# Attention with a threshold on the weights: a float32 screen without a norm check, GpSimd with DMA alone, flags and split in one instruction each

## The chip, the cores and the metric

The kernel runs on one core of a Trainium2 chip. The metric is the device time of one execution in microseconds, as the median of several runs. A NeuronCore has TensorE (PE, with its weight loads as PEld), VectorE (DVE), ScalarE (ACT), GpSimd (POOL) and SyncE (SP), which work side by side, each through its instructions in order, and wait for one another by semaphores. [...]

## The reference

```
Q, K, V: (8, 12, 512, 64) float32, normally distributed; threshold = 0.1
scores  = einsum('bhqd,bhkd->bhqk', Q, K) / sqrt(64)
weights = softmax(scores)
weights = where(weights > threshold, weights, 0)
weights = weights / (sum(weights) + 1e-10)
out     = einsum('bhqk,bhkd->bhqd', weights, V)
```

A query row in which no weight is over 0.1 gives a row of zeros.

## The kernel before

Two heads make a pair, and there are 48 pairs. A tile of a pair has 128 partitions; Q and K of both heads lie side by side as 128 columns, 4 rows a partition. SyncE first writes zeros into the whole output of a pair (L173). The kernel then screens all query rows at low cost, finds those in which a weight can pass the threshold, and computes only these rows exactly and writes them over the zeros.

A pair goes through these steps, in five turns of the loop over pairs:

1. *Load and transpose.* `do_load` fetches Q, K and V (three pairs ahead). `do_tr` (L182) transposes Q and K by 4 float32 matmuls each; ScalarE takes Q out of PSUM as bf16 (`do_qev`, L188) and K as float32 with its row sums (`do_kev`, L194); VectorE writes 512 times K minus its sum as bf16 (`do_kcentre`, L200).
2. *Screen.* Four steps `g` a pair: `do_qk` (L231) makes the scores of 128 rows of both heads by two matmuls, head 0 on rows 0 to 63 of the array, head 1 on rows 64 to 127. `do_screen` gives head 0 to ScalarE, a sum of exponentials (L243), and head 1 to VectorE, a maximum (L245).
3. *Norms.* GpSimd squares the bf16 Q and K (`do_squares`, L208), TensorE sums the squares (`do_norms`, L217), ScalarE keeps them (`do_normev`, L222). At the end the largest norm tells whether the bf16 screen's margin was wide enough.
4. *Select.* `do_flags` (L250, L251) compares sums and maxima with a cut. `do_rank` (L259, L261) counts flagged rows by matmuls, `do_key` and `do_idx` turn the counts into row numbers, and `do_gather` (L287) fetches up to 64 rows of each head by an indirect DMA of GpSimd.
5. *Exact rows.* `do_split` (L297, two instructions) puts the rows of the two heads into separate columns, `do_xtr` (L303) transposes, `do_xqk` (L314) makes float32 scores, `do_xexp` (L320) the exponentials, `do_xmask` (L326, L328) the threshold, `do_xpt` (L336) the transpose of the weights, `do_xptev` (L342) its eviction by ScalarE, `do_xpv` (L351) the product with V, whose 65th column of ones gives the sum; `do_xout` scales (L358 to L361) and scatters the rows by an indirect DMA of GpSimd (L362). V is cast to bf16 by VectorE (`do_vcast`, L177).

The order of each engine is the program's own: every instruction is pinned by `keep(...)`, and the loop over `g` at the end of the function writes the steps of five pairs in one fixed order, by `qi`, the step within the pair. For pair `hp`, TensorE's order is: score pair 0, rank of `hp-1`, transposes of Q of `hp+1`, L314 of `hp-3`, score pair 1, transposes of K of `hp+1`, L351 of `hp-4`, score pair 2, row numbers of `hp-1`, score pair 3, L303, L336, norms. The scores, the transposes and L314 share 5 PSUM buffers (`spsum`).

If more than 64 rows of a head are flagged, or a norm is too large, a slow loop at the end (L465 on) computes everything; it is not entered here.

Of the kernel before, what the change touches and what calls it, by code (L numbers as in the profile page):

```python
# [11 lines left out]
def kernel(  # L12
# [33 lines left out]
    DV = D + 1  # L46
# [15 lines left out]
    SCREEN = mybir.dt.bfloat16  # L62
    NORM_CAP = 160.0

    MARGIN = 1.05 * NORM_CAP * 2.0 ** -8 * scale + 0.005
# [80 lines left out]
    load = ctx.enter_context(tc.tile_pool(name="load", bufs=5))  # L146
    tpool = ctx.enter_context(tc.tile_pool(name="t", bufs=3))
# [9 lines left out]
    q_in, k_in, v_in, q_t, k_t, kc_t = {}, {}, {}, {}, {}, {}  # L157
# [4 lines left out]
    def load_pair(q_sb, k_sb, v_sb, hp):  # L162
        for dst, src in ((q_sb, Qf), (k_sb, Kf)):
            for h2 in range(2):
                nc.sync.dma_start(out=dst[:, :, h2 * D:(h2 + 1) * D], in_=src[hp][:, :, h2, :])
        nc.sync.dma_start(out=v_sb[:], in_=Vf[hp])

    def do_load(hp):
        q_sb = load.tile([P, SO, 2 * D], f32)
        k_sb = load.tile([P, SO, 2 * D], f32)  # L170
        v_sb = load.tile([P, 2, SO, D], f32)
        load_pair(q_sb, k_sb, v_sb, hp)
        nc.sync.dma_start(out=Oz[hp], in_=zero[:])  # L173
        q_in[hp], k_in[hp], v_in[hp] = q_sb, k_sb, v_sb

    def do_vcast(hp):
        keep(nc.vector.tensor_copy(v_bufs[hp % NV][:, :, :, 0:D], v_in.pop(hp)[:]))  # L177

# [7 lines left out]
    def do_qev(hp, sc):  # L186
        qt = tpool.tile([P, SO * P], SCREEN)
        keep(nc.scalar.copy(qt[:], sc[:]))  # L188
        q_t[hp] = qt

    def do_kev(hp, sc):
# [19 lines left out]
    def do_norms(hp):  # L211
        nm = mpsum.tile([P, P], f32, name="sm")
        for which in range(2):
            sq = sq_t.pop((hp, which))
            for r in range(SO):
                c = (which * SO + r) * 2
                keep(nc.tensor.matmul(nm[:, c:c + 2], lhsT=sq[:, r * P:(r + 1) * P], rhs=heads[:],  # L217
                                      start=True, stop=True))
        nm_t[hp] = nm

    def do_normev(hp):
        keep(nc.scalar.copy(norms[:, hp].rearrange("p w c -> p (w c)"), nm_t.pop(hp)[:, 0:4 * SO]))  # L222
# [3 lines left out]
    def do_qk(g):  # L226
        hp, qi = divmod(g, SO)
        for h2 in range(2):
            sc = spsum.tile([P, SO * P], f32)
            ps = slice(h2 * D, (h2 + 1) * D)  # L230
            keep(nc.tensor.matmul(sc[:], lhsT=q_t[hp][ps, qi * P:(qi + 1) * P],  # L231
                                  rhs=kc_t[hp][ps, :], start=True, stop=True))
            sc_t[g, h2] = sc

    def do_screen(g):
        hp, qi = divmod(g, SO)
        if qi == 0:
            sums = small.tile([P, SO], f32)
            tops = small.tile([P, SO], f32)
            st_t[hp] = sums, tops  # L240
        sums, tops = st_t[hp]
        junk = junkp.tile([P, SO * P], bf16)
        keep(nc.scalar.activation(junk[:], sc_t.pop((g, 0))[:], ACTF.Exp, scale=BETA * scale / CS,  # L243
                                  accum_out=sums[:, qi:qi + 1]))
        keep(nc.vector.tensor_reduce(tops[:, qi:qi + 1], sc_t.pop((g, 1))[:], axis=AX.X, op=ALU.max))  # L245
# [47 lines left out]

    def do_split(hp):
        qb = work.tile([P, 2 * D], f32)
        for h2 in range(2):
            keep(nc.vector.tensor_scalar(qb[:, h2 * D:(h2 + 1) * D], qsel_bufs[hp % NS][:],  # L297
                                         half[:, h2:h2 + 1], None, op0=ALU.mult))
        qb_t[hp] = qb

    def do_xtr(hp):
        xp = mpsum.tile([P, P], f32, name="sm")
        keep(nc.tensor.matmul(xp[:], lhsT=qb_t.pop(hp)[:], rhs=identity_f32[:],  # L303
# [36 lines left out]
    def do_xptev(hp):  # L340
        pt = work.tile([P, SO, P], bf16)
        keep(nc.scalar.copy(pt[:], ptp_t.pop(hp)[:]))  # L342
        pts_t[hp] = pt

    def do_xpv(hp):
        pt = pts_t.pop(hp)
        o = mpsum.tile([P, P], f32, name="sm")
        for h2 in range(2):
            sl = slice(h2 * SLOTS, (h2 + 1) * SLOTS)
            for kj in range(SO):  # L350
                keep(nc.tensor.matmul(o[sl, 0:DV], lhsT=pt[:, kj, sl], rhs=v_bufs[hp % NV][:, h2, kj, :],  # L351
                                      start=(kj == 0), stop=(kj == SO - 1)))
        o_t[hp] = o
# [188 lines left out]
```

## Time and profile before

| | us |
|---|---|
| median of 3 runs | 572.74 |
| lowest, highest | 569.52, 573.75 |
| the profiled execution | 567.96 |
| its span in the profile | 566.2 |

The profile is of one execution. Busy time is given by engine and line; the idle time before an instruction is put down to what released it. A time in order of time counts from the span's start. TensorE's ends are modelled, and GpSimd's spans are rough.

### The profile page before, as it was taken

The numbers are of one execution on the slowest core, as the hardware profiler recorded it, in microseconds if no ns is written. First come the engines' busy times: TensorE is split into PE (matmuls) and PEld (weight loads), VectorE is DVE, ScalarE is ACT, GpSimd is POOL, SyncE is SP. The second block draws the span as 40 slices with busy tenths as digits, with TensorE's granted clock in tenths as the row PEclk, the third lists the DMA queues.
The fourth block names the chain that finished last, engine by engine and source line by source line (L and its number), as shares of the span: only waits on it lengthen the run. The fifth ranks groups of instructions, "written<-read, shape, count | busy, mean of one in ns | idle before, by whom it ended". The sixth has DMA issues, their size and how long they took to land. (4 is left out here: it accounts for less than half of the span.)

```text
span 566.2 us, 7626 instructions
## 1 busy us (share of the span) xinstructions
PE 353.7 (62%) x2258; PEld 180.1 (32%) x2258; DVE 396.6 (70%) x873; ACT 255.5 (45%) x769; POOL 202.1 (36%) x224
## 2 busy tenths in 40 slices
PE   4766665675666656567665775667565775567561
PEld 2332333233333332333332332333232333233220
DVE  2866778577777776786787667776777678766841
ACT  4544544454445434544544445435544454444430
POOL 5432344223433432352244223432334224432421
PEclk9766566666665666766566657566756656665655
DMA  7982444244344333433432244334433342000000
GB/s 196 264 203 69 114 114 115 68 117 102 78 106 119 81 78 92 125 89 88 120 97 79 78 121 106 79 76 108 115 84 77 87 117 64 23 21 4 2 6 3
DMA packets 124460, 52.13 MB, mean 92 GB/s; under 512 B 104764, under 2 KB 118272, under 8 KB 124416
## 3 DMA queue, kind: packets, MB, share of 16 engines
q1 hardware_dynamic: 121344, 50.35, 34.0%
q0 software_dynamic: 3072, 1.27, 1.3%
q8 instruction: 19, 0.31, 0.2%
q14 instruction: 25, 0.20, 0.1%
HBM read 39.32 MB, written 14.16 MB: 94 GB/s over the span
## 5 line engine op out<-in xcount | busy, mean ns | idle before, releaser
L245 DVE TENSOR_REDUCE tops<-sc 128x1 f32<-128x512 f32 x192 | 131.7, 686 | 135.0 <-PE sc L231 135.0
L287 POOL DMA_INDIRECT qsel<-in_Q_dram,idx x48 | 51.6, 1074 | 288.2 <-DVE idx L286 228.6
L243 ACT ACTIVATE junk<-sc 128x512 bf16<-128x512 f32 x192 | 114.0, 600 | 75.2 <-PE sc L231 75.1
L251 DVE TENSOR_SCALAR f<-tops 128x4 bf16<-128x4 f32 x48 | 115.6, 2408 | 0.0
L231 PE MATMUL sc<-kc,qt 64*128 64x512 bf16 x384 | 100.8, 518 | 2.3 <-DVE kc L200 2.3
L314 PE MATMUL sc<-kt,xq 128*128 128x512 f32 x96 | 92.5, 1067 | 0.0
L188 ACT CAST qt<-sc 128x512 bf16<-128x512 f32 x48 | 28.1, 586 | 125.5 <-PE sc L182 125.5
L303 PE MATMUL sm<-identity_f,qb 128*128 128x128 f32 x48 | 21.0, 438 | 88.4 <-DVE qb L297 82.9
L259 PE MATMUL sm<-f,tri 128*128 128x8 bf16 x48 | 9.0, 188 | 100.1 <-DVE f L251 100.1
L362 POOL DMA_INDIRECT out_dram<-res,idx x48 | 48.7, 1015 | 59.0 <-ACT xq L309 47.0
L182 PE MATMUL sc<-identity_f,q_sb 128*128 128x128 f32 x192 | 52.5, 429 | 4.9 <-POOL qsel L143 4.9
L208 POOL TENSOR_TENSOR sq<-qt 128x512 bf16<-128x512 bf16 x48 | 50.3, 1048 | 4.4 <-ACT qt L188 3.2
L208 POOL TENSOR_TENSOR sq<-kc 128x512 bf16<-128x512 bf16 x48 | 50.0, 1041 | 2.8 <-DVE kc L200 2.8
L182 PE MATMUL sc<-identity_f,k_sb 128*128 128x128 f32 x192 | 46.1, 385 | 0.5 <-DMA k_sb<-in_K_dram 0.5
L231 PEld LDWEIGHTS <-qt 64*128 64x128 bf16 x384 | 19.6, 98 | 76.2 <-issue 72.5
L259 PEld LDWEIGHTS <-tri 128*128 128x128 bf16 x48 | 5.0, 104 | 120.5 <-DVE f L251 119.4
L303 PEld LDWEIGHTS sm<-identity_f,qb 128*128 128x128 f32 x48 | 8.2, 171 | 104.8 <-DVE qb L297 102.9
L309 ACT COPY xq<-sm 128x128 f32<-128x128 f32 x48 | 12.8, 266 | 60.4 <-PE sm L303 60.4
L243 ACT ACTIVATION_READ_ACCUMULATOR junk<-sc 128x1 f32 x192 | 39.1, 204 | 0.0
L328 DVE SCALAR_TENSOR_TENSOR m<-e,tv 128x512 bf16<-128x512 f32 x48 | 36.1, 751 | 1.7
L182 PEld LDWEIGHTS sc<-identity_f,k_sb 128*128 128x128 f32 x192 | 30.4, 196 | 19.6 <-issue 19.2
L182 PEld LDWEIGHTS sc<-identity_f,q_sb 128*128 128x128 f32 x192 | 34.4, 217 | 5.3 <-POOL qsel L143 4.9
(63 smaller groups left out, 464.4 us busy)
## 6 DMA issues: line engine op xcount, KB each, us to landing
q_sb<-in_Q_dram SPq DMA_DIRECT2D x96, 128.0 KB, 3.5
k_sb<-in_K_dram SPq DMA_DIRECT2D x96, 128.0 KB, 3.3
v_sb<-in_V_dram SPq DMA_DIRECT2D x48, 256.0 KB, 3.5
out_dram<-zero SPq DMA_DIRECT2D x48, 256.0 KB, 3.3
qsel<-in_Q_dram,idx POOLq DMA_INDIRECT x48, 4.6
out_dram<-res,idx POOLq DMA_INDIRECT x48, 2.2
```

What stands on the lines that cost most here:

```text
L182: keep(nc.tensor.matmul(sc[:, r * P:(r + 1) * P], lhsT=src[:, r, :], rhs=identity_f32[:], is_transpose=True, start=True, stop=True))
L188: keep(nc.scalar.copy(qt[:], sc[:]))
L208: keep(nc.gpsimd.tensor_tensor(out=sq[:], in0=src[:], in1=src[:], op=ALU.mult))
L231: keep(nc.tensor.matmul(sc[:], lhsT=q_t[hp][ps, qi * P:(qi + 1) * P], rhs=kc_t[hp][ps, :], start=True, stop=True))
L243: keep(nc.scalar.activation(junk[:], sc_t.pop((g, 0))[:], ACTF.Exp, scale=BETA * scale / CS, accum_out=sums[:, qi:qi + 1]))
L245: keep(nc.vector.tensor_reduce(tops[:, qi:qi + 1], sc_t.pop((g, 1))[:], axis=AX.X, op=ALU.max))
L251: keep(nc.vector.tensor_scalar(f[:, 1, :], tops[:], CUT * CS / scale, None, op0=ALU.is_gt))
L287: keep(nc.gpsimd.indirect_dma_start(out=qsel_bufs[hp % NS][:], out_offset=None, in_=Qr, in_offset=bass.IndirectOffsetOnAxis(ap=idx[:, 0:1] ...
L303: keep(nc.tensor.matmul(xp[:], lhsT=qb_t.pop(hp)[:], rhs=identity_f32[:], is_transpose=True, start=True, stop=True))
L314: keep(nc.tensor.matmul(sc[:], lhsT=xq_t.pop(hp)[:], rhs=k_t.pop(hp)[:], start=True, stop=True))
L328: keep(nc.vector.scalar_tensor_tensor(out=m[:], in0=e[:], scalar=tv[:, 0:1], in1=e[:], op0=ALU.is_gt, op1=ALU.mult))
L362: keep(nc.gpsimd.indirect_dma_start(out=Or, out_offset=bass.IndirectOffsetOnAxis(ap=ix_t.pop(hp)[:, 0:1], axis=0), in_=res[:], in_offset=N ...
```

## The change

- The screen's Q and centred K become float32 and lie in one tile `qk`; the score matmuls are float32. The margin of the cut is 0.01, and the norms, their squares and their check at the end are left out.
- GpSimd's loop holds only DMAs: the gather, the scatter, and a DMA that loads V two pairs ahead and casts it to bf16 (`do_vload`). SyncE no longer loads V, VectorE no longer casts it.
- The screen of step 3 is done by ScalarE for both heads, so VectorE takes 3 maxima a pair instead of 4, ScalarE 5 exponentials instead of 4.
- The flags are one comparison of two tiles, the split one product of two broadcast tiles.
- The eviction of the transposed weights goes from ScalarE to VectorE, the scaling of the result from VectorE to ScalarE.
- V has no column of ones any more: four more matmuls with one column each make the sum.

```diff
...
-    SCREEN = mybir.dt.bfloat16
-    NORM_CAP = 160.0
-
-    MARGIN = 1.05 * NORM_CAP * 2.0 ** -8 * scale + 0.005
+    SCREEN = f32
+    MARGIN = 0.01
...
+    cuts = consts.tile([P, 2, SO], f32)
+    nc.gpsimd.memset(cuts[:], CUT_SUM)
+    nc.gpsimd.memset(cuts[:, 1, 0:SO - 1], CUT * CS / scale)
...
+    vpool = ctx.enter_context(tc.tile_pool(name="v", bufs=8))
...
-        nc.sync.dma_start(out=v_sb[:], in_=Vf[hp])
+
+    def do_vload(hp):
+        v_bf = vpool.tile([P, 2, SO, D], bf16)
+        keep(nc.gpsimd.dma_start(out=v_bf[:], in_=Vf[hp]))
+        v_in[hp] = v_bf
...
-    def do_vcast(hp):
-        keep(nc.vector.tensor_copy(v_bufs[hp % NV][:, :, :, 0:D], v_in.pop(hp)[:]))
...
-        qt = tpool.tile([P, SO * P], SCREEN)
-        keep(nc.scalar.copy(qt[:], sc[:]))
-        q_t[hp] = qt
+        qk = tpool.tile([P, 2, SO * P], SCREEN)
+        keep(nc.scalar.copy(qk[:, 0, :], sc[:]))
+        qk_t[hp] = qk
...
-    def do_squares(hp, which):
-        sq = work.tile([P, SO * P], bf16, name=f"sq{which}")
-        src = q_t[hp] if which == 0 else kc_t[hp]
-        keep(nc.gpsimd.tensor_tensor(out=sq[:], in0=src[:], in1=src[:], op=ALU.mult))
-        sq_t[hp, which] = sq
...
-            keep(nc.tensor.matmul(sc[:], lhsT=q_t[hp][ps, qi * P:(qi + 1) * P],
-                                  rhs=kc_t[hp][ps, :], start=True, stop=True))
+            keep(nc.tensor.matmul(sc[:], lhsT=qk_t[hp][ps, 0, qi * P:(qi + 1) * P],
+                                  rhs=qk_t[hp][ps, 1, :], start=True, stop=True))
...
+        for h2 in range(2):
+            sc = sc_t.pop((g, h2))
+            if h2 == 0 or qi == SO - 1:
+                junk = junkp.tile([P, SO * P], bf16)
+                keep(nc.scalar.activation(junk[:], sc[:], ACTF.Exp, scale=BETA * scale / CS,
+                                          accum_out=stat[:, h2, qi:qi + 1]))
+            else:
+                keep(nc.vector.tensor_reduce(stat[:, h2, qi:qi + 1], sc[:], axis=AX.X, op=ALU.max))
...
-        keep(nc.vector.tensor_scalar(f[:, 0, :], sums[:], CUT_SUM, None, op0=ALU.is_gt))
-        keep(nc.vector.tensor_scalar(f[:, 1, :], tops[:], CUT * CS / scale, None, op0=ALU.is_gt))
+        keep(nc.vector.tensor_tensor(out=f[:], in0=st_t.pop(hp)[:], in1=cuts[:], op=ALU.is_gt))
...
-        for h2 in range(2):
-            keep(nc.vector.tensor_scalar(qb[:, h2 * D:(h2 + 1) * D], qsel_bufs[hp % NS][:],
-                                         half[:, h2:h2 + 1], None, op0=ALU.mult))
+        keep(nc.vector.tensor_tensor(
+            out=qb[:], in0=qsel_bufs[hp % NS][:].unsqueeze(1).to_broadcast([P, 2, D]),
+            in1=half[:].unsqueeze(2).to_broadcast([P, 2, D]), op=ALU.mult))
...
-        keep(nc.scalar.copy(pt[:], ptp_t.pop(hp)[:]))
+        keep(nc.vector.tensor_copy(pt[:], ptp_t.pop(hp)[:]))
...
+        for kj in range(SO):
+            keep(nc.tensor.matmul(o[:, D:D + 1], lhsT=pt[:, kj, :], rhs=ones_bf[:, 0:1],
+                                  start=(kj == 0), stop=(kj == SO - 1)))
...
-        keep(nc.vector.tensor_scalar(res[:], o[:, 0:D], rcp[:, 0:1], None, op0=ALU.mult))
+        keep(nc.scalar.activation(res[:], o[:, 0:D], ACTF.Copy, scale=rcp[:, 0:1]))
...
-            if has(hp):
-                do_norms(hp)
+            if has(hp + 2):
+                do_vload(hp + 2)
...
```

VectorE, around the flags of a pair. Before, from the split (`qb`) over the scaling (`res`) and the fourth maximum (`tops`) to the two flag instructions (`f`), the next pair's first maximum and the cast of V:

```order
L297 TENSOR_SCALAR qb<-qsel_111,half 128x64 x2
L358 TENSOR_SCALAR rcp<-sm 128x1
L359 RECIPROCAL rcp<-rcp 128x1
L361 TENSOR_SCALAR res<-sm,rcp 128x64
L245 TENSOR_REDUCE tops<-sc 128x1
L250 TENSOR_SCALAR f<-sums 128x4
L251 TENSOR_SCALAR f<-tops 128x4
L245 TENSOR_REDUCE tops<-sc 128x1
L177 CAST v_one_99<-v_sb 128x8x64
```

In the changed kernel, the same place:

```order
L264 TENSOR_TENSOR qb<-qsel_93,half 128x128
L329 TENSOR_SCALAR rcp<-sm 128x1
L330 RECIPROCAL rcp<-rcp 128x1
L218 TENSOR_TENSOR f<-stat,cuts 128x8
L214 TENSOR_REDUCE stat<-sc 128x1
L310 COPY pt<-pt 128x512
```

The scaling and the fourth maximum have gone from between the reciprocal and the flags, the split and the flags are one instruction each, and the eviction of the weights (`pt`) stands where the cast of V stood.

ScalarE, from the eviction of K (`kt`) to the next pair's first screen (`junk`), before:

```order
L194 ACTIVATE kt,ksum<-sc 128x512
L320 ACTIVATE e,sum_4590<-sc 128x512
L243 ACTIVATE junk,sums<-sc 128x512 x2
L309 COPY xq<-sm 128x128
L222 COPY norms<-sm 128x16
L243 ACTIVATE junk,sums<-sc 128x512
```

In the changed kernel, from the exponentials of the exact rows (`e`) on:

```order
L288 ACTIVATE e,sum_4202<-sc 128x512
L211 ACTIVATE junk,stat<-sc 128x512
L332 ACTIVATE res<-sm,rcp 128x64
L211 ACTIVATE junk,stat<-sc 128x512 x2
L277 COPY xq<-sm 128x128
L211 ACTIVATE junk,stat<-sc 128x512
```

The scaling (`res`) now stands between the third screen and the last one, which has two instructions.

GpSimd, one pair and the start of the next, before, with the gather (`qsel`), the scatter (`out_dram`) and the squares (`sq`):

```order
L287 DMA qsel_109<-in_Q_dram,idx 128x64
L362 DMA out_dram<-res,idx 49152x64
L208 TENSOR_TENSOR sq_2448<-qt 128x512
L208 TENSOR_TENSOR sq_2480<-kc 128x512
L287 DMA qsel_111<-in_Q_dram,idx 128x64
```

In the changed kernel:

```order
L254 DMA qsel_93<-in_Q_dram,idx 128x64
L333 DMA out_dram<-res,idx 49152x64
L157 DMA v_bf<-in_V_dram 128x2x256
L254 DMA qsel_95<-in_Q_dram,idx 128x64
L333 DMA out_dram<-res,idx 49152x64
```

The load of V stands where the squares stood.

## Rows read from the trace of the kernel before

**Rows 1.** Busy time of each engine, share of the span, instructions.

```profile
PE 353.7 (62%) x2258; PEld 180.1 (32%) x2258; DVE 396.6 (70%) x873; ACT 255.5 (45%) x769; POOL 202.1 (36%) x224
```

**Rows 2.** Line L251 (min/median/max, first and last start), and the wait for it.

```profile
L251 DVE TENSOR_SCALAR f<-tops x48: 157/2768/2778, 14.9 to 538.5; 128x4 bf16<-128x4 f32 x48
...
PE sm L259 <- DVE f L251: 100.1, 45, 2.5
```

**Rows 3.** Order of time around the flags: start us, us, engine, line, operation [idle before].

```profile
308.24 1.02 POOL L362 DMA_INDIRECT out_dram<-res,idx  x1 [1.11 <-ACT xq L309]
...
308.59 2.77 DVE L251 TENSOR_SCALAR f<-tops 128x4 bf16<-128x4 f32 x1
...
309.28 1.05 POOL L208 TENSOR_TENSOR sq<-qt 128x512 bf16<-128x512 bf16 x1
...
310.28 1.04 POOL L208 TENSOR_TENSOR sq<-kc 128x512 bf16<-128x512 bf16 x1
...
311.42 0.19 PE L259 MATMUL sm<-f,tri 128*128 128x8 bf16 x1 [2.49 <-DVE f L251]
```

**Rows 4.** Order of time, flags of the last pair.

```profile
537.45 1.02 POOL L362 DMA_INDIRECT out_dram<-res,idx  x1 [0.31 <-DVE res L361]
...
538.49 0.16 DVE L251 TENSOR_SCALAR f<-tops 128x4 bf16<-128x4 f32 x1
```

**Rows 5.** Order of time, TensorE: a dense stretch, and a score pair of another.

```profile
322.90 1.09 PE L182 MATMUL sc<-identity_f,q_sb 128*128 128x128 f32 x4
323.79 1.92 PE L314 MATMUL sc<-kt,xq 128*128 128x512 f32 x2
325.63 0.61 PE L231 MATMUL sc<-kc,qt 64*128 64x512 bf16 x2
...
327.22 0.44 PE L351 MATMUL sm<-v_one,pt 128*64 128x65 bf16 x8
...
315.89 0.39 PE L231 MATMUL sc<-kc,qt 64*128 64x512 bf16 x2
```

**Rows 6.** Order of time, VectorE, from the third maximum to the reciprocal.

```profile
304.99 0.69 DVE L245 TENSOR_REDUCE tops<-sc 128x1 f32<-128x512 f32 x1 [0.74 <-PE sc L231]
...
306.96 0.41 DVE L297 TENSOR_SCALAR qb<-qsel,half 128x64 f32<-128x64 f32 x2
...
307.47 0.16 DVE L359 RECIPROCAL rcp<-rcp 128x1 f32<-128x1 f32 x1
```

**Rows 7.** Stretches: length, busy us (x) of PE, PEld, DVE, ACT, POOL; granted clock, DMA, GB/s.

```profile
299.40:305.10 5.70, 5.61 (x32) 2.83 (x32) 2.26 (x7) 2.82 (x7) 0.00 (x0) 0.50 0.40 125
305.10:308.50 3.40, 1.31 (x19) 0.83 (x17) 3.30 (x12) 1.64 (x8) 1.32 (x2) 1.00 0.49 108
308.50:312.00 3.50, 1.01 (x8) 0.59 (x7) 3.50 (x5) 0.85 (x3) 2.80 (x3) 0.50 0.03 7
...
323.60:329.00 5.40, 5.37 (x26) 2.08 (x24) 1.97 (x6) 3.44 (x10) 0.00 (x0) 0.50 0.55 153
...
14.90:538.50 523.60, 335.49 (x2162) 171.55 (x2161) 384.20 (x833) 244.33 (x742) 188.57 (x184) 0.62 0.36 94
...
315.60:316.00 0.40, 0.40 (x11) 0.31 (x10) 0.36 (x3) 0.34 (x2) 0.00 (x0) 1.00 1.06 384
```

**Rows 8.** Groups by line: busy us, mean ns | idle before; L177 as min/median/max.

```profile
L243 ACT ACTIVATE junk<-sc 128x512 bf16<-128x512 f32 x192 | 114.0, 600 | 75.2 <-PE sc L231 75.1
...
L243 ACT ACTIVATION_READ_ACCUMULATOR junk<-sc 128x1 f32 x192 | 39.1, 204 | 0.0
...
L361 DVE TENSOR_SCALAR res<-sm,rcp 128x64 f32<-128x64 f32 x48 | 13.6, 283 | 1.6
...
L177 DVE CAST v_one<-v_sb x48: 411/415/2505, 10.1 to 531.1; 128x512 bf16<-128x512 f32 x48
```

**Rows 9.** Line L328 (min/median/max ns), and a gather beside it.

```profile
L328 DVE SCALAR_TENSOR_TENSOR m<-e,tv x48: 750/752/753, 36.2 to 552.0; 128x512 bf16<-128x512 f32 x48
...
306.07 1.05 POOL L287 DMA_INDIRECT qsel<-in_Q_dram,idx  x1 [6.68 <-DVE idx L286]
```

More of the change, by code (lines that the diff above doesn't have):

```diff
@@ L195, in do_kev @@
         k_t[hp] = kt
-        kc_t[hp] = ksum
+        ks_t[hp] = ksum
     def do_kcentre(hp):
-        kc = tpool.tile([P, SO * P], SCREEN)
-        keep(nc.vector.tensor_scalar(kc[:], k_t[hp][:], CS, kc_t[hp][:, 0:1],
+        keep(nc.vector.tensor_scalar(qk_t[hp][:, 1, :], k_t[hp][:], CS, ks_t.pop(hp)[:, 0:1],
                                      op0=ALU.mult, op1=ALU.subtract))
-        kc_t[hp] = kc
-    def do_squares(hp, which):
-        sq = work.tile([P, SO * P], bf16, name=f"sq{which}")
-        src = q_t[hp] if which == 0 else kc_t[hp]
-        keep(nc.gpsimd.tensor_tensor(out=sq[:], in0=src[:], in1=src[:], op=ALU.mult))
-        sq_t[hp, which] = sq
[L211 to L222, printed above, removed]
     sc_t = {}
@@ L237, in do_screen @@
         if qi == 0:
[L238 to L245, printed above, removed]
+            stat = small.tile([P, 2, SO], f32)
+            st_t[hp] = stat
+        stat = st_t[hp]
+        for h2 in range(2):
[6 more added lines that the diff above has]
+                keep(nc.vector.tensor_reduce(stat[:, h2, qi:qi + 1], sc[:], axis=AX.X, op=ALU.max))
     def do_flags(hp):
-        sums, tops = st_t.pop(hp)
         f = small.tile([P, 2, SO], bf16)
-        keep(nc.vector.tensor_scalar(f[:, 0, :], sums[:], CUT_SUM, None, op0=ALU.is_gt))
-        keep(nc.vector.tensor_scalar(f[:, 1, :], tops[:], CUT * CS / scale, None, op0=ALU.is_gt))
+        keep(nc.vector.tensor_tensor(out=f[:], in0=st_t.pop(hp)[:], in1=cuts[:], op=ALU.is_gt))
         f_t[hp] = f
@@ L302, in do_xtr @@
         xp = mpsum.tile([P, P], f32, name="sm")
[L303 removed]
+        keep(nc.tensor.matmul(xp[:], lhsT=qb_t.pop(hp)[:].rearrange("p h d -> p (h d)"), rhs=identity_f32[:],
                               is_transpose=True, start=True, stop=True))
@@ L368 @@
         do_load(hp)
+    for hp in range(2):
+        do_vload(hp)
     do_qev(0, do_tr(q_in.pop(0)))
@@ L414 @@
                 do_xexp(hp - 3)
-            if has(hp):
-                do_squares(hp, 1)
         elif qi == 2:
@@ L436 @@
                 do_xpt(hp - 3)
-            if has(hp):
-                do_norms(hp)
+            if has(hp + 2):
+                do_vload(hp + 2)
             if g < G:
@@ L442 @@
                 do_xev(hp - 2)
-            if has(hp):
-                do_normev(hp)
-    most = small.tile([P, 3], f32)
-    nc.vector.tensor_reduce(most[:, 0:1], keys[:].rearrange("p n c -> p (n c)"), axis=AX.X, op=ALU.max)
-    for which, unit in ((0, NORM_CAP), (1, NORM_CAP * CS * CS)):
-        nc.vector.tensor_reduce(most[:, 1 + which:2 + which], norms[:, :, which, :], axis=AX.XY, op=ALU.max)
-        nc.vector.tensor_scalar(most[:, 1 + which:2 + which], most[:, 1 + which:2 + which],
-                                1.01 * (SLOTS + 0.5) / unit, None, op0=ALU.mult)
     over = small.tile([P, 1], f32)
-    nc.vector.tensor_reduce(over[:], most[:], axis=AX.X, op=ALU.max)
+    nc.vector.tensor_reduce(over[:], keys[:].rearrange("p n c -> p (n c)"), axis=AX.X, op=ALU.max)
     over_t = mpsum.tile([P, P], f32, name="sm")
@@ L468 @@
             k_sb = load.tile([P, SO, 2 * D], f32)
-            v_sb = load.tile([P, 2, SO, D], f32)
-            load_pair(q_sb, k_sb, v_sb, hp)
-            v_one = v_bufs[0]
-            nc.vector.tensor_copy(v_one[:, :, :, 0:D], v_sb[:])
+            v_bf = vpool.tile([P, 2, SO, D], bf16)
+            load_pair(q_sb, k_sb, hp)
+            nc.gpsimd.dma_start(out=v_bf[:], in_=Vf[hp])
             qt = ktpool.tile([P, SO * P], f32, name="kt")
@@ L498 @@
                     for kj in range(SO):
-                        nc.tensor.matmul(o[:, 0:DV], lhsT=pt[:, kj, :], rhs=v_one[:, h2, kj, :],
+                        nc.tensor.matmul(o[:, 0:D], lhsT=pt[:, kj, :], rhs=v_bf[:, h2, kj, :],
+                                         start=(kj == 0), stop=(kj == SO - 1))
+                    for kj in range(SO):
+                        nc.tensor.matmul(o[:, D:D + 1], lhsT=pt[:, kj, :], rhs=ones_bf[:, 0:1],
                                          start=(kj == 0), stop=(kj == SO - 1))
                     rcp = small.tile([P, 1], f32)
-                    nc.vector.tensor_scalar_add(rcp[:], o[:, D:DV], 1e-10)
+                    nc.vector.tensor_scalar_add(rcp[:], o[:, D:D + 1], 1e-10)
                     nc.vector.reciprocal(rcp[:], rcp[:])
```

31 lines of the change are left out of this document (8 added, 23 removed).

## The prediction

> **What bounds the kernel now.** I read the shares of the engines first: VectorE is busy for 70% of the span and TensorE for 62% [rows 1], at a mean granted TensorE clock of 0.62 between the first and the last pair [rows 7]. No engine is full, so I asked what each pair waits for. Of 566.2 us, 523.6 lie between the first and the last flag instruction, 47 pairs apart; that is 11.14 us for a pair, and 42.6 us lie before and after [rows 2].
>
> The list of waits names a chain at once: the rank matmul (L259) waited 100.1 us for the flag instruction of L251, in 45 of 48 pairs. L251 compares 4 elements a partition, which takes 0.157 us at its shortest; its median is 2.77 us [rows 2]. The order of time says why: L251 starts at 308.59, while GpSimd is in a scatter (L362) behind which the two squaring multiplies of L208 stand. L251 ends at 311.36, just as the second square ends at 311.32, and L259 starts 0.06 us later [rows 3]. For the last pair, where no squares follow the scatter, L251 takes 0.16 us beside the end of a scatter [rows 4]. So it is the squares that hold VectorE, 2.6 us a pair, and TensorE with it.
>
> The rest of a pair is two stretches. In the dense one, from L259 to the third score pair, TensorE works nearly without a break (5.61 of 5.70 us at granted clock 0.50). In the tail a chain on VectorE runs to the flags, and TensorE is busy for only 1.31 of 3.40 us [rows 7]. The clock rose to 1.00 after the full stretch and fell back to 0.50 after the sparse one [rows 7].
>
> **The change, part by part.**
>
> *The squares go.* The 48 flag instructions of L251 cost 2.77 us where the squares run and 0.16 us where they do not [rows 3, 4]: 2.6 us a pair leave the chain, if nothing else on GpSimd holds VectorE. I take that. What is late next is the score chain worked out below.
>
> *The score matmuls become float32.* This is the price. [...] If a constant part a stays and the streaming s halves, s = 0.44 and a = 0.17. The nearest float32 row is L314, also 512 columns: it is split into two passes, together 1.92 us, so s = 1.75 at the lower level and, if it halves as the bf16 one does, 0.87 at the upper; no row shows it there. A new pair is two such matmuls on the two halves of the rows. If the halves still run beside each other, as the two bf16 ones do, a pair streams 1.75 or 0.87 us; if not, twice that. I take the overlap. Its nearest row is L351: 8 matmuls of 65 columns, first four on one half of the columns, then four on the other, in 0.44 us. In turn they would take 8 x 65/512 x 0.44 + 0.17 = 0.62; in pairs 0.40 [rows 5]. So the engine paired work that is not adjacent in the program.
>
> [...]
>
> *The dense stretch*, with streaming times: rank 0.2, four transposes of Q 0.92 (1.09 less 0.17), L314 1.75, a score pair 1.75, four of K 0.92, L351 with its four new matmuls 0.4 (0.27 + half as much), a score pair 1.75, three changes of row tiling at 0.1 (from 323.79 + 1.75 to 325.63), and 0.27 to VectorE's start: 8.26 us at the lower level, 4.7 at the upper (transposes and long matmuls halved) [rows 3, 5]. How much of it runs at which level is the choice: the clock rises after a full stretch and falls after a sparse one [rows 7], and this stretch begins after a tail. At the lower level it would now last 8.26 us and not 5.5 (two bf16 pairs at 0.44, no new matmuls), so the rise comes inside it, and the rest is at the upper level. I take seven tenths of the work there: 4.7 + 0.3 x 3.56 = 5.8 us. Ends: 4.7 and 8.26.
>
> *The tail.* Before, the third maximum starts at 304.99 and the second reciprocal step ends at 307.63: 2.64 us [rows 6]. The split becomes one instruction instead of two, which between them took 0.41 [rows 6]: 2.45 remain. Now the scaling moves to ScalarE, between the third and the last screen, so the two last exponentials wait for it, and the flags wait for them: 0.28 (as L361 took on VectorE), two at 0.6 by L243, 0.2 to read the sum, 0.16 for the flags and some 0.2 of handing over [rows 3, 8]. Sum 4.4 us. Before, without the stall, it was 3.8 (304.99 to 308.59 + 0.16) [rows 3, 6]; so 0.6 us come back here. The fourth and the next first score pair lie inside this chain at the upper level; at the lower they stretch it to some 5.0.
>
> *Off the path.* The P-transpose's eviction leaves ScalarE for VectorE, between 0.41 (the cast it loses) and 0.69 (a maximum, also out of PSUM); it falls into the dense stretch, where VectorE is busy 2.26 of 5.70 us [rows 6 to 8]. Without that cover it would cost its 0.5. The centring now writes float32, between the same ends, and stays in the tail's 2.64 us; I take no change. The cast of V, the norm matmuls and their eviction go from covered places. V by a GpSimd DMA has no row; the nearest is an indirect one, 1.05 us [rows 9]. It is queued behind the scatter and ahead of the next gather; the data is used four pairs later and the gather a pair later, so I take nothing, from 0 to 1.05.
>
> *Sum.* 5.8 + 4.4 = 10.2 us a pair. The same working gives for before 5.5 at the lower level, 3.2 at the upper, and 6.4 of tail with the stall (304.99 to 311.42): 11.9 or 9.6, and the mean of 11.14 lies between. Then 47 x 10.2 + 42.6 = 522.0 us of span, and with the 1.8 us between span (566.2) and profiled execution (567.96) 524 us. The median shown is 572.74, 0.8% above that execution; the sum is left on the execution's scale.
>
> **The rivals.**
>
> *Three passes a pair.* The halves overlap only in the middle. The dense stretch's two score pairs grow by half: 0.87 each at the lower, 0.44 at the upper level, 1.1 us mixed. 11.3 us a pair, 576 us: nothing won. For it: float32 is split in two passes for each half, and they stand in turn. Against: L351 [rows 5].
>
> *No overlap at all (slower).* Float32 passes on half the rows run one after another. Dense 8.26 + 3.5 = 11.8 us at the lower level, 6.4 at the upper, mixed 8.0; the tail then ends with TensorE: 2.2 to the split, some 0.9 of transposes (five, at 0.23 or half of it) and a first score pair of 1.8 to 3.5, some 5.4. 13.4 us, 674 us; at the lower level alone some 900. It decides from the point where a pair of score matmuls takes over 3 us. For it: no row shows float32 on half the rows. Against: bf16 does it in every pair [rows 5].
>
> *Overlap, but the clock stays low (slower).* 8.26 + 5.0 = 13.3 us, 669 us. The rise at 305.10 speaks against it [rows 7].
>
> *The stall stays (slower).* The flags now read two SBUF inputs, and GpSimd has a third DMA to prepare. If that holds VectorE as the squares did, 2.4 us a pair return (2.6 in 45 of 48 [rows 2]): 12.6 us, 637 us. Against: L328, with two inputs in SBUF, lasts 750 to 753 ns in all 48 pairs, also where a gather runs beside it [rows 9].
> [...]
>
> **How the numbers follow.** Forecast 0.70: 524 us, own range 472 (all upper: 4.7 + 4.4 = 9.1) to 557 (half of the stretch at each level, 6.5 + 4.4 = 10.9). Three passes 0.10, no overlap 0.10, low clock 0.05, stall 0.05. A measurement of this kernel tells about 1% from no change. The three passes split into 0.04 faster, 0.03 same, 0.03 slower, so faster is 0.74, same 0.03, slower 0.23. The range reaches from 455, which leaves 0.35 us a pair below all upper for the unpriced VectorE pieces, to 620, which takes in the three passes with 44 us to spare and leaves out no overlap, the low clock and the stall: 0.20.
>
> **What would show it.** Right: the flag instruction at some 0.2 us with no wait of L226 on it of 2 us; two score matmuls of different halves starting within 0.1 us; a granted clock well over 0.62; some 10 us a pair. Wrong: the second half starting after the first one's two passes, or a clock of 0.5 throughout; a flag or centring instruction over 1 us beside a GpSimd DMA; or TensorE waiting for ScalarE's last two exponentials for more than the tail's 4.4 us.

## The result, and the profile after

| | before, us | after, us |
|---|---|---|
| median | 571.13 (4 runs, 564.54 to 573.75) | 466.71 (4 runs, 466.27 to 470.94) |
| span of the profiled execution | 566.2 | 464.7 |
| granted TensorE clock over that span, share of full speed | 0.625 | 0.975 |

The ratio is 0.822, 95% interval 0.8125 to 0.8314. The forecast was 524 us, the range 455 to 620: the sign is right and the time lies in the range, but the gain is more than twice the one forecast: 104 us between the medians, where the forecast had 44 on the scale of the profiled execution. In three of the runs below one execution of four had a lower clock and took longer (422.05, 535.42 and 557.25 us); the ratios are of the others.

The page of the kernel after: busy time of each engine, and the clock in 40 slices of the span, in tenths.

```profile
PE 376.2 (81%) x2450; PEld 165.2 (36%) x2450; DVE 230.3 (50%) x676; ACT 258.9 (56%) x817; POOL 140.6 (30%) x169
...
PEclk9999999999999999999999999999999999999955
```

VectorE, the busiest in [rows 1], is down to 50%. TensorE is the busiest now, but its busy time grew by only 22.5 us on [rows 1], although its score matmuls are float32: the clock is at its upper level, 1.00, from the first slice to the end of the last pair; its lower level is 0.50. In [rows 7] the mean was 0.62.

The flag line (minimum, median, maximum in ns, first and last start), and what TensorE and the flags waited for (us in total, times, longest):

```profile
L218 DVE TENSOR_TENSOR f<-stat,cuts x48: 166/167/169, 18.0 to 439.3; 128x8 bf16<-128x8 f32 x48
...
DVE f L218 <- ACT junk L211: 71.6, 48, 1.5
...
PE sm L226 <- DVE f L218: 17.3, 45, 1.4
```

The stall of [rows 2] is gone in all 48 pairs: 0.167 us for a median of 2.768, and the rank matmul's wait fell from 100.1 to 17.3 us. What the flags now wait for is ScalarE's last exponential. From the first flag to the last there are 421.3 us, 8.96 a pair; 43.4 us lie outside (42.6 before). The first three pairs and the last are shorter; a steady pair takes 9.12 us.

One steady pair, cut as in the prediction: the dense stretch from the rank matmul to the third score pair's maximum, then the tail to the next rank matmul (columns as in [rows 7]).

```profile
304.15:308.98 4.83, 4.83 (x38) 2.33 (x38) 2.06 (x6) 2.97 (x10) 0.66 (x1) 1.00 0.69 141
308.98:313.27 4.29, 2.82 (x18) 1.04 (x16) 2.68 (x10) 2.38 (x9) 2.17 (x3) 1.00 0.27 60
```

Both run at 1.00. In order of time, the same pair's TensorE work and the end of its tail:

```profile
304.27 0.64 PE L170 MATMUL sc<-identity_f,q_sb 128*128 128x128 f32 x4
...
304.74 1.02 PE L282 MATMUL sc<-kt,xq 128*128 128x512 f32 x2
...
305.69 1.13 PE L197 MATMUL sc<-qk 64*128 64x512 f32 x4
...
310.95 0.28 DVE L264 TENSOR_TENSOR qb<-qsel,half 128x128 f32<-128x128 f32 x1
...
311.30 0.33 PE L271 MATMUL sm<-identity_f,qb 128*128 128x128 f32 x1 [1.11 <-DVE qb L264]
...
311.54 0.32 ACT L332 ACTIVATE res<-sm,rcp 128x64 f32<-128x64 f32 x1 [1.92 <-DVE rcp L330]
311.75 0.59 ACT L211 ACTIVATE junk<-sc 128x512 bf16<-128x512 f32 x1
...
312.32 0.60 ACT L211 ACTIVATE junk<-sc 128x512 bf16<-128x512 f32 x1
...
313.04 0.17 DVE L218 TENSOR_TENSOR f<-stat,cuts 128x8 bf16<-128x8 f32 x1 [1.54 <-ACT junk L211]
...
313.15 0.78 POOL L157 DMA_DIRECT2D v_bf<-in_V_dram  x1
```

The float32 score pair's four passes take 1.13 us, little more than the two passes of L282, 1.02 us: the halves overlap. Transposes and L282 take little more than half of what [rows 5] show for them (1.09 and 1.92 us). The tail ends as forecast: scaling, two exponentials, flags. TensorE's longest wait in the pair is 1.11 us; in [rows 3] it was 2.49.

### The profile page after: what moved, and what is told of

Read it like the earlier page. It is cut to its first block, busy times and chain, and to the rows that moved or that the text cites. A ratio compares the mean times of both kernels' runs of the same rounds, so it can differ in the third digit from the quotient of the medians.

```text
span 464.7 us, 7628 instructions
## 1 busy us (share of the span) xinstructions
PE 376.2 (81%) x2450; PEld 165.2 (36%) x2450; DVE 230.3 (50%) x676; ACT 258.9 (56%) x817; POOL 140.6 (30%) x169
## 5 line engine op out<-in xcount | busy, mean ns | idle before, releaser
L197 PE MATMUL sc<-qk 64*128 64x512 f32 x768 | 219.2, 646 | 1.7 <-DVE qk L187 1.7
L211 ACT ACTIVATE junk<-sc 128x512 bf16<-128x512 f32 x240 | 143.3, 601 | 81.4 <-PE sc L197 81.1
L214 DVE TENSOR_REDUCE stat<-sc 128x1 f32<-128x512 f32 x144 | 99.2, 689 | 132.7 <-PE sc L197 132.7
L197 PEld LDWEIGHTS sc<-qk 64*128 64x128 f32 x768 | 58.7, 186 | 46.3 <-issue 35.6
L271 PE MATMUL sm<-identity_f,qb 128*128 128x128 f32 x48 | 16.1, 334 | 52.3 <-DVE qb L264 52.3
L282 PE MATMUL sc<-kt,xq 128*128 128x512 f32 x96 | 51.4, 618 | 0.0
L271 PEld LDWEIGHTS sm<-identity_f,qb 128*128 128x128 f32 x48 | 6.7, 140 | 90.5 <-DVE qb L264 90.5
L157 POOL DMA_DIRECT2D v_bf<-in_V_dram x48 | 37.4, 780 | 1.2 <-PE sc L170 1.2
L176 ACT COPY qk<-sc 128x512 f32<-128x512 f32 x48 | 28.1, 586 | 17.2 <-PE sc L170 16.9
L288 ACT ACTIVATE e<-sc 128x512 f32<-128x512 f32 x48 | 28.7, 597 | 5.7 <-PE sc L282 5.7
L182 ACT ACTIVATE kt<-sc 128x512 f32<-128x512 f32 x48 | 28.3, 589 | 0.7 <-PE sc L170 0.7
L187 DVE TENSOR_SCALAR qk<-kt,ksum 128x512 f32<-128x512 f32 x48 | 22.9, 477 | 6.5 <-ACT kt L182 6.5
```

The lines of the kernel that those rows point to most:

```text
L157: keep(nc.gpsimd.dma_start(out=v_bf[:], in_=Vf[hp]))
L176: keep(nc.scalar.copy(qk[:, 0, :], sc[:]))
L182: keep(nc.scalar.activation(kt[:], sc[:], ACTF.Copy, accum_out=ksum[:]))
L197: keep(nc.tensor.matmul(sc[:], lhsT=qk_t[hp][ps, 0, qi * P:(qi + 1) * P], rhs=qk_t[hp][ps, 1, :], start=True, stop=True))
L211: keep(nc.scalar.activation(junk[:], sc[:], ACTF.Exp, scale=BETA * scale / CS, accum_out=stat[:, h2, qi:qi + 1]))
L214: keep(nc.vector.tensor_reduce(stat[:, h2, qi:qi + 1], sc[:], axis=AX.X, op=ALU.max))
```

## Experiments

Two explanations stood against each other for the gain beyond the forecast: the float32 matmuls themselves keep the clock up, or the stall's end does. The first five runs change the type of the screen, the number of its matmuls or the squares, in the kernel after or in the one before. The others take the tail, the order and the squares' place apart. Ratios are to the kernel before on the same chip. A line of three dots marks what a diff or a list leaves out.

### The screen in bf16, in the kernel after

```diff
-    SCREEN = f32
-    MARGIN = 0.01
+    SCREEN = bf16
+    MARGIN = 1.05 * 160.0 * 2.0 ** -8 * scale + 0.005
```

> The changed kernel with the screen's Q and centred K as bf16 again, under the old margin (so some more rows are flagged; the 64 slots are the same). Theory 1, the float32 matmuls are what keeps the TensorE clock up: the granted clock falls to 0.6 to 0.8, the dense stretch lies between 3.2 us (upper level) and 5.5 (lower), with the tail of 4.4 that is 8.5 to 9.5 us a pair, 444 to 491 us, about as long as the float32 kernel (467). Theory 2, the clock rose because the squares' stall is gone and TensorE no longer pauses: the clock stays above 0.9 and the pair falls to some 8.0 us, 420 us.

Measured: 486.48 us, ratio 0.8589 (0.8536 to 0.8641), clock 0.639, as the first theory said. The cheaper matmuls make the kernel 20 us slower, although the stall is gone. The page's clock line, then the dense stretch and the tail of one pair of 9.98 us, all of it at 0.50, and TensorE's work in it (other pairs are at both levels, 8.97 us at 0.69):

```profile
PEclk9998665666656666556675577655666656666555
```

```profile
207.16:212.85 5.69, 5.68 (x34) 2.90 (x34) 2.07 (x5) 2.90 (x9) 0.67 (x1) 0.50 0.52 119
212.85:217.14 4.29, 2.14 (x14) 0.86 (x13) 2.68 (x10) 2.44 (x11) 2.17 (x3) 0.50 0.30 66
...
208.18 1.91 PE L282 MATMUL sc<-kt,xq 128*128 128x512 f32 x2
...
210.02 0.61 PE L197 MATMUL sc<-qk 64*128 64x512 bf16 x2
...
215.17 0.47 PE L271 MATMUL sm<-identity_f,qb 128*128 128x128 f32 x1 [1.62 <-DVE qb L264]
```

A bf16 pair at the lower level (0.61 us) still beats a float32 pair at the upper (1.13), but L282, which the change does not touch, goes from 1.02 to 1.91 us, and the transposes with it. The tail is as long as that of after, 4.29 us, but TensorE is busy for 2.14 us of it, not 2.82, and waits 1.62 us for the split, not 1.11.

### The same, with every bf16 score matmul issued twice

```diff
...
+            sc_t[g, h2] = sc
+        for h2 in (0, 1, 0, 1):
+            sc = sc_t[g, h2]
+            ps = slice(h2 * D, (h2 + 1) * D)
             keep(nc.tensor.matmul(sc[:], lhsT=qk_t[hp][ps, 0, qi * P:(qi + 1) * P],
                                   rhs=qk_t[hp][ps, 1, :], start=True, stop=True))
-            sc_t[g, h2] = sc
```

> The bf16 screen in the kernel after (486.5 us, granted clock 0.64) with every bf16 score matmul issued twice into the same tile: pure extra work for TensorE, four matmuls of 512 columns a quarter, the norm check absent as in after. Theory (float32 beats bf16 here because a busier TensorE is granted the upper level): the clock rises to over 0.8 and the time falls below 480 us although work was added. Rival (the slow bf16 run has another cause, the extra matmuls only cost): the clock stays near 0.64 and 4 pairs of 0.4 to 0.6 us are added, over 560 us.

Measured: 472.53 us, ratio 0.8281 (0.8251 to 0.8312), clock 0.808. The theory holds: pure extra work made the kernel 14 us faster than the bf16 screen. So in this order the clock rose with the work that TensorE was given, from 0.639 to 0.808; nothing else differs between these two runs, the margin included.

### Before without squares and norms

The norm check at the end, which the diff leaves out, goes too.

```diff
...
-                do_squares(hp, 0)
...
-                do_squares(hp, 1)
...
-                do_norms(hp)
...
-                do_normev(hp)
...
```

> The kernel before without its squares, norm matmuls, norm evictions and norm check (the check of the bf16 margin is left out), nothing else. If the squares alone held the flags: L251 at 0.16 us in all pairs and 2.4 us less a pair, 8.7 us, 455 us, at a clock of 0.6 to 0.7 (theory 1) or above 0.9 with some 7.6 us a pair, 402 us (theory 2). If something else on GpSimd holds VectorE, L251 stays over 1 us and the time over 500.

Measured: 404.36 us, ratio 0.7115 (0.7054 to 0.7177), clock 0.858. The clock lies between the two theories, the time is near the second's 402 us. L251 takes 0.170 us in the median. This part of the change alone gains 163 us on its own chip's before (567.42), more than the whole change: 3.5 us a pair, of which the stall explains 2.6. Half of its pairs take 7.0 us at the upper level, the others 8.2 to 8.5 us at 0.75 to 0.84. A pair at the upper level:

```profile
283.32:286.49 3.17, 3.13 (x26) 1.60 (x26) 2.01 (x5) 2.49 (x8) 0.44 (x1) 1.00 0.30 60
286.49:290.32 3.83, 1.49 (x14) 0.77 (x14) 3.72 (x15) 2.54 (x10) 1.60 (x2) 1.00 0.82 232
```

The tail is the 3.8 us that the prediction gave for before without the stall. The dense stretch, with bf16 scores, is the 3.2 us that it gave at the upper level.

### Before with a float32 screen

```diff
-    SCREEN = mybir.dt.bfloat16
+    SCREEN = f32
```

> The kernel before with nothing changed but the type of the screen's tiles: float32 score matmuls, the squares taken of float32 tiles, norms and norm check as before. It asks what the float32 screen brings while GpSimd still multiplies. Theory (the squares hold the flags and TensorE idles behind them, whatever the type): dense stretch some 5.0 us at the upper clock level plus the tail with the stall, 6.4 us: 11.2 to 11.6 us a pair, 560 to 590 us, at a clock above 0.75 if the longer matmuls hold it. Rival (float32 scores alone buy the clock and with it most of the gain): under 520 us. Rival 2 (the clock stays near 0.62 because of the idle tail): over 620 us.

Measured: 667.95 us, ratio 1.1677 (1.161 to 1.1743), clock 0.759. The time is in the second rival's range, but not for its reason, a clock near 0.62 throughout; the theory was 78 us short. The dense stretch and the tail of one pair, and then, in order of time, the flags and what follows them:

```profile
412.16:419.38 7.22, 7.22 (x34) 3.23 (x34) 2.06 (x5) 3.02 (x8) 0.00 (x0) 0.62 0.39 109
419.38:425.81 6.43, 3.16 (x26) 1.34 (x24) 6.32 (x14) 2.50 (x8) 4.11 (x4) 0.90 0.20 45
```

```profile
409.33 2.77 DVE L251 TENSOR_SCALAR f<-tops 128x4 bf16<-128x4 f32 x1
...
412.16 0.19 PE L259 MATMUL sm<-f,tri 128*128 128x8 bf16 x1 [1.91 <-DVE f L251]
...
413.17 1.91 PE L314 MATMUL sc<-kt,xq 128*128 128x512 f32 x2
...
415.02 2.08 PE L231 MATMUL sc<-kc,qt 64*128 64x512 f32 x4
...
418.18 1.13 PE L231 MATMUL sc<-kc,qt 64*128 64x512 f32 x4
```

The tail with the stall is the forecast 6.4 us. But TensorE stands 1.91 us for the flags, and comes out at the lower level: L314 takes 1.91 us, the first score pair 2.08, and only the second is back at 1.13. The dense stretch is 7.22 us where after has 4.83. So the stall costs twice: its own length, and the clock of what follows. Here float32 matmuls do not hold the clock over the wait.

### Before without squares and norms, screen in float32

```diff
-    SCREEN = mybir.dt.bfloat16
+    SCREEN = f32
...
-    MARGIN = 1.05 * NORM_CAP * 2.0 ** -8 * scale + 0.005
+    MARGIN = 0.01
```

on the kernel of the third run.

> The kernel before with the squares, the norm matmuls, their eviction and the norm check left out, and the screen in float32; everything else of the change left out. It prices the float32 screen alone against the run without the norms (404.4 us). Theory: the float32 matmuls add their streaming to the dense stretch (4.83 us in after against 3.17 at the upper clock level without norms, less some 0.2 for the four new matmuls) and hold the clock up, while the tail stays at 3.83 us: some 8.4 us a pair, 430 to 445 us. Rival 1 (the clock gives back what the streaming costs): 404 us or less. Rival 2 (the float32 screen is the whole difference between 404 and 467): 460 us or more.

Measured: 445.46 us, ratio 0.7793 (0.7771 to 0.7816), clock 0.973; 8.65 us a pair. Dense stretch and tail of one:

```profile
298.42:303.08 4.66, 4.66 (x35) 2.17 (x34) 2.21 (x5) 3.55 (x10) 0.28 (x1) 1.00 0.47 128
303.08:307.07 3.99, 2.79 (x17) 1.07 (x17) 3.67 (x13) 1.64 (x5) 1.75 (x2) 1.00 0.54 124
```

The theory's account holds, half a microsecond above its range: the tail came out 0.16 us longer than 3.83.

| | bf16 screen | float32 screen |
|---|---|---|
| squares and norms in | 571 us, clock 0.62 | 668 us, clock 0.76 |
| squares and norms out | 404 us, clock 0.86 | 445 us, clock 0.97 |

Without the squares, float32 costs 41 us; with them, 97. Dropping the squares is worth 167 us with bf16 and 222 with float32, that is 3.5 and 4.7 us a pair for a stall of 2.6. The clock is near its upper level throughout only where both the stall is gone and the screen is float32.

### The tail of after back on VectorE

```diff
...
-            if h2 == 0 or qi == SO - 1:
+            if h2 == 0:
...
-        keep(nc.scalar.activation(res[:], o[:, 0:D], ACTF.Copy, scale=rcp[:, 0:1]))
+        keep(nc.vector.tensor_scalar(res[:], o[:, 0:D], rcp[:, 0:1], None, op0=ALU.mult))
```

> The kernel after with the last screen of head 1 back on VectorE as a maximum and the scaling of the result back on VectorE. It undoes only the part of the change that lengthened the tail. Theory: the two exponentials in turn behind a scaling on ScalarE cost 0.5 us a pair against one maximum and one scaling on VectorE (tail 4.29 us in after, 3.83 in the run without norms at the upper clock level, 0.2 less here for the merged split): 8.5 us a pair, 435 to 447 us. Rival (VectorE's two more instructions of 0.28 and 0.69 us stand in the same chain and cost as much as they free): 460 to 470 us.

Measured: 446.44 us, ratio 0.7814 (0.7787 to 0.784), clock 0.971, in the theory's range. Dense stretch and tail:

```profile
298.56:303.39 4.83, 4.83 (x40) 2.33 (x38) 2.21 (x5) 3.10 (x10) 1.07 (x2) 1.00 0.62 130
303.39:307.25 3.86, 2.75 (x17) 1.04 (x17) 3.50 (x11) 1.60 (x5) 1.77 (x2) 1.00 0.41 87
```

The dense stretch is that of after; the tail is 3.86 us instead of 4.29. Moving the scaling and the last screen to ScalarE costs 20 us. This kernel differs from the one above (445.46) by V's DMA, the merged flags and split, the eviction on VectorE and the four matmuls for the sum; together these change the time by no more than 1 us. That is a balance: the dense stretch is 0.17 us longer than above, where the four matmuls stand, and the tail 0.13 us shorter, where the split is one instruction.

### The scaling earlier, and the scores ahead

The scaling first: `do_xout` is called ahead of `do_kcentre` in step 2 of the pair.

```diff
...
             if has(hp - 1):
                 do_gather(hp - 1)
+            if has(hp - 4):
+                do_xout(hp - 4)
             if has(nxt):
                 do_kcentre(nxt)
...
-            if has(hp - 4):
-                do_xout(hp - 4)
```

> The changed kernel with the scaling of the result (two reciprocal steps, the product on ScalarE, the scatter) placed before the centring instead of after the split. ScalarE then no longer waits for VectorE's chain before the two last exponentials. If the tail is set by reciprocal, scaling, two exponentials, flags: the rank starts some 0.4 us earlier a pair (then after the split, two transposes and the first score pair), 8.7 us, 447 us. If the flags were covered anyway: 467 within 1%.

Measured: 464.57 us, ratio 0.8177 (0.812 to 0.8233), clock 0.961. That is 0.5% less than after, no gain to speak of: the forecast of 447 us failed. A pair takes mostly 8.94 us, 0.18 less than 9.12, but four of the 47 take 10.54 us. In those the clock falls, and a score pair takes 1.86 to 2.04 us for 1.13, so that the mean pair is 8.92 us for 8.96. In order of time, that score pair in one of the four; then, in a steady pair, the flags, which are no longer what the rank waits for:

```profile
218.73 2.03 PE L197 MATMUL sc<-qk 64*128 64x512 f32 x4
...
309.26 0.33 PE L271 MATMUL sm<-identity_f,qb 128*128 128x128 f32 x1 [1.36 <-DVE qb L264]
...
309.30 0.17 DVE L218 TENSOR_TENSOR f<-stat,cuts 128x8 bf16<-128x8 f32 x1
...
309.74 1.13 PE L197 MATMUL sc<-qk 64*128 64x512 f32 x4
310.81 0.18 PE L226 MATMUL sm<-f,tri 128*128 128x8 bf16 x1
```

The flags are done at 309.47, but the rank starts at 310.81: ahead of it on TensorE stand L271, which waits for the split, and the next pair's scores. So the next run also issues those scores ahead of L271 and L304:

```diff
...
-        if g < G:
+        if g < G and (qi != 0 or g == 0):
             do_qk(g)
...
         else:
+            if g + 1 < G:
+                do_qk(g + 1)
             if has(hp - 2):
                 do_xtr(hp - 2)
```

> The kernel after, with the scaling moved up (as in the run with the scaling early) and the next pair's first two float32 score matmuls put ahead of the transposes of the chosen queries and of P, so that they no longer wait for VectorE's split. Theory (the pair's length of 9.12 us is the dense stretch of 4.8 us plus a tail that is a chain through VectorE, TensorE and ScalarE, and the score matmuls stand inside that chain behind the split): the last screen starts earlier and the tail loses what the split holds, 0.8 to 1.3 us a pair; 410 to 435 us. Rival (the ScalarE queue sets the tail, with its scaling and two last exponentials): no more than 0.2 us a pair comes off the 464.6 us of the run with the scaling early; 455 to 465 us.

Measured: 411.59 us, ratio 0.7206 (0.7164 to 0.7247), clock 0.975, 7.88 us a pair, in the theory's range. It computes what after computes and beats both kernels.

```profile
PE 367.3 (90%) x2450; PEld 165.9 (41%) x2450; DVE 233.5 (57%) x676; ACT 262.0 (64%) x817; POOL 150.1 (37%) x169
```

TensorE is busy for 90% of the span. Here the scaling and the two exponentials on ScalarE, which cost 20 us in after, are no longer alone in the tail: TensorE has the next scores to do beside them.

The same order with the screen in bf16:

```diff
-    SCREEN = f32
-    MARGIN = 0.01
+    SCREEN = bf16
+    MARGIN = 1.05 * 160.0 * 2.0 ** -8 * scale + 0.005
```

> The run with the scores ahead (411.6 us, 7.88 us a pair, float32), with its screen in bf16 and the wider margin; the norm check is absent as in after. Theory (TensorE's clock follows the work it is given, so the shorter matmuls lose the upper level): the clock falls below 0.85 and the time is no better than 400 us, between 400 and 440. Rival (with the scores ahead TensorE has no long gap left, so the clock stays at its upper level and the streaming saved counts, some 1.2 us a pair): 345 to 365 us.

Measured: 386.62 us, ratio 0.6737 (0.6681 to 0.6792), clock 0.799 in the profiled execution and up to 0.822 in the others. The clock fell as the theory said, but the time is below its range and above the rival's. Inside a pair the clock is at both levels:

```profile
201.41 1.92 PE L282 MATMUL sc<-kt,xq 128*128 128x512 f32 x2
...
203.25 0.61 PE L197 MATMUL sc<-qk 64*128 64x512 bf16 x2
...
204.93 0.39 PE L197 MATMUL sc<-qk 64*128 64x512 bf16 x2
```

So bf16 loses the clock's upper level here too (0.799, where float32 in this order has 0.975), and loses less by it than it saves in streaming: 386.62 us against 411.59. That bf16 is slower than float32 belongs to the order of after, not to the types. Without a norm check this screen's margin rests on norms below the cap of 160, so it is no substitute for after.

### The squares back in the kernel after

Squares of the float32 tiles on GpSimd, their sums and the check left out. First behind V's DMA:

```diff
+    def do_squares(hp, which):
+        sq = work.tile([P, SO * P], bf16, name=f"sq{which}")
+        src = qk_t[hp][:, which, :]
+        keep(nc.gpsimd.tensor_tensor(out=sq[:], in0=src, in1=src, op=ALU.mult))
...
+                do_squares(hp, 0)
...
+                do_squares(hp, 1)
```

> The changed kernel with the two squares of Q and centred K of each pair on GpSimd at their old places in the order, from the float32 tiles; their sums and the check stay out. If the squares hold VectorE whatever the form of the flag instruction: the flag instruction L218 (here a few lines lower) at 2 us or more, 11 to 11.7 us a pair, 560 to 590 us, and the clock still above 0.8. If one instruction with two inputs is not held: 467 us within 2%.

Measured: 509.95 us, ratio 0.8977 (0.8919 to 0.9035), clock 0.923. That lies between the two forecasts. The flag's median is 0.588 us, not the 2.77 of [rows 2]:

```profile
L223 DVE TENSOR_TENSOR f<-stat,cuts x48: 167/588/2216, 16.7 to 485.0; 128x8 bf16<-128x8 f32 x48
...
312.03 0.59 DVE L223 TENSOR_TENSOR f<-stat,cuts 128x8 bf16<-128x8 f32 x1 [1.54 <-ACT junk L216]
312.13 0.79 POOL L157 DMA_DIRECT2D v_bf<-in_V_dram  x1
...
312.91 2.08 POOL L193 TENSOR_TENSOR sq<-qk 128x512 bf16<-128x512 f32 x2
```

V's DMA stands between the scatter and the squares, so that the flags are over before the squares begin. The 0.42 us by which the flags are longer make 20 of the 43 us to after: most pairs take 9.54 us for 9.12. Most of the rest comes from a dozen pairs of some 11 us, with the clock at 0.85. The longest flag, 2.216 us, is that of the last pair but one, at 472.23: no V is left to load there, and the squares follow the scatter directly. To tell whether the merged flag instruction is immune or was only lucky in its place, V's DMA went behind the second square:

```diff
                 do_squares(hp, 1)
+            if has(hp + 2):
+                do_vload(hp + 2)
...
-            if has(hp + 2):
-                do_vload(hp + 2)
```

> The run with the squares put back into the kernel after (510.0 us, flags of 0.59 us), with V's GpSimd DMA moved behind the second square, so that the squares follow the scatter directly, as in before; their sums and the norm check are left out. It asks whether the merged flag instruction, with two inputs in SBUF, escapes the squares, or only stood ahead of them because V's DMA came first. Theory (the squares hold whatever VectorE does beside them): the flag instruction takes over 2 us, TensorE idles for it, the clock falls with it below 0.9, and the time is 590 to 670 us. Rival (the merged form is not held by the squares): flags under 0.7 us and 470 to 515 us.

Measured: 667.84 us, ratio 1.1717 (1.168 to 1.1755), clock 0.758. The theory holds.

```profile
L223 DVE TENSOR_TENSOR f<-stat,cuts x48: 155/2216/2667, 17.6 to 643.4; 128x8 bf16<-128x8 f32 x48
```

```profile
414.72:421.92 7.20, 7.20 (x38) 3.20 (x38) 2.06 (x5) 2.53 (x8) 0.61 (x1) 0.64 0.43 95
...
425.99 2.22 DVE L223 TENSOR_TENSOR f<-stat,cuts 128x8 bf16<-128x8 f32 x1 [1.53 <-ACT junk L216]
426.12 2.06 POOL L193 TENSOR_TENSOR sq<-qk 128x512 bf16<-128x512 f32 x2
428.10 0.79 POOL L157 DMA_DIRECT2D v_bf<-in_V_dram  x1
...
428.27 0.19 PE L231 MATMUL sm<-f,tri 128*128 128x8 bf16 x1 [2.42 <-DVE f L223]
```

The merged instruction is held like the old one, 2.2 us, until the squares end at 428.18. The place of one DMA in GpSimd's queue is worth 158 us between these two runs. A steady pair takes 13.65 us here and 9.54 there: 1.63 of the 4.1 us is the flag's own length (2.216 less 0.588), and 2.37 is the dense stretch behind the wait, 7.20 us at a clock of 0.64 here and 4.83 at 1.00 there. In before with a float32 screen it was 7.22.

## Why the prediction was right or wrong

**The squares hold the flags (right).** The flag instruction went to 0.167 us and TensorE's wait went with it. The run with the squares directly behind the scatter brings 2.2 us back, the one with them behind V's DMA does not. Both are without the norm matmuls, so it is the multiplies themselves: 2.22 us beside L193.

**Float32 halves overlap (right).** Four passes take 1.13 us, against 1.02 for the two of L282. Three passes would add half of L282's streaming, some 0.4 us. The rival's three passes do not fit the 1.13 us.

**The two stretches at the upper level (right).** Forecast 4.7 and 4.4 us, measured 4.83 and 4.29. Their sum, 9.1, is the end "all upper" of the forecast's own range, and it is what a steady pair takes: 9.12 us.

**The share of the upper level (wrong: the step that failed).** The prediction put it: "I take seven tenths of the work there: 4.7 + 0.3 x 3.56 = 5.8 us." Measured: all of it, 4.83 us. The 0.97 us between are 46 of the 58 us by which 524 exceeds the profiled execution's 466; 0.11 us of tail make 5, and the shorter pairs at the ends (8.96 on average, not 9.12) some 7.5. The reason given was that "this stretch begins after a tail", and that the clock had fallen after the sparse tail of before. But that tail had the stall (1.01 us busy in the 3.50 us behind 308.50, [rows 7]) and bf16 scores, and the change takes away both. The prediction left their mark on the clock in place.

Neither alone is enough. Without the stall, but with bf16 scores, the dense stretch in the order of after runs whole pairs at the lower level: 5.69 us at 0.50. With float32 scores, but with the stall, it takes 7.22 us at 0.62; the rise inside the stretch that the prediction described exists there. With both it takes 4.83 us at 1.00. What in the tail decides is open: TensorE is busy for 2.82 of its 4.29 us in after and for 2.14 of as many with bf16, and no run takes the busy time and the waits apart.

**The price of float32 (right as a length, incomplete as a price).** The prediction's s and a are worked out from what a bf16 pair takes at the two levels of the clock, 0.61 us at 0.50 and 0.39 at 1.00 [rows 5, 7]; the bf16 run with the scores ahead shows the same two times. The streaming of float32 costs 41 us without the squares. In after it is paid back by the clock: the bf16 screen there takes 486.48 us. The prediction's sum had no term by which more TensorE work could save time: it let the longer dense stretch bring the rise, but nothing keep the level through the tail.

**ScalarE's tail comes back (right, but smaller).** Forecast: 4.4 us of tail for 3.8, so 0.6 us a pair, in which the merged split had already saved 0.2; like for like that is 0.8. Measured with the split merged in both: 0.43 us (4.29 and 3.86), 20 us in all. The terms that the prediction lists for the tail add up to 4.49 us, not 4.4. With that the forecast would be 528 us, and the miss a little larger.

**Nothing off the path (right).** V's DMA takes 0.78 us, the eviction on VectorE 0.41; with the merged flags, the split and the four matmuls they change the time by at most 1 us, 446.44 against 445.46. The split's saving and the four matmuls' cost are both in the prediction's terms, and they cancel. V is used six turns of the loop after its load, not four; TensorE does not wait for it.

**The rivals.** Three passes and no overlap fall by the 1.13 us, the low clock by 0.975, the stall that stays by 0.167 us. The last one's price, 637 us, was too low for the reason for which the forecast was too high: it left the clock as it was. With a stall of 2.2 us the kernel after takes 667.84.

What 571 became 467 by, in steps that were each run: float32 screen, +97; squares, norms and check out, -222; V's DMA, the merged instructions, the eviction and the four matmuls, +1; scaling and last screen to ScalarE, +20. The first two depend on their order: with the squares out first they are -167 and +41.

## What to carry to other kernels

When a stall on TensorE's path goes, the clock that it cost may come back, as it did here with float32 scores (a dense stretch of 7.20 us at 0.64 with the squares behind the scatter, 4.83 at 1.00 without them): read the granted clock of the stretch that follows the wait, and price the matmuls there at both levels (L282 is 1.02 or 1.91 us). Do not carry the level of the old kernel over into the new sum, and do not count on the rise either: here it took the longer matmuls too. A change that lessens TensorE's work can cost time: with bf16 scores in the order of after it waits 1.62 us for the split, not 1.11, the granted clock is 0.639, not 0.975, and the kernel is 20 us slower. In the order with the scores ahead bf16 is the faster one. Before a GpSimd multiply is blamed or cleared, look at what stands beside it: one DMA ahead of it in the queue was worth 158 us.

## What the runs showed of the hardware that was not expected

- In the order of after, the kernel is faster with float32 scores than with bf16 ones (466.7 and 486.5 us), and faster with every bf16 matmul doubled than with each once (472.5 and 486.5 us), by a granted clock of 0.975, 0.808 and 0.639.
- TensorE came out of a 1.91 us wait at 0.50 even with float32 scores; in the steady pair of after, with no wait over 1.11 us, it stayed at 1.00. In the pair with bf16 scores, with waits of 1.62 and 0.53 us, it was at 0.50 throughout.
- With the squares queued behind V's DMA the flags last 0.588 us and end inside that DMA; in after, where the DMA starts just as soon beside them (0.11 us after their start, 0.10 there), they last 0.167. Why is open: the squares queued behind the DMA are what differs, but the flags end before they start.
